# Hybrid decoder trunk: where the FFN's weight sums and work tiles stand in SBUF, the order inside a seven-product chunk, and an eighth seven-product group per layer

## The chip, the core and the metric

The kernel runs on one core of one Trainium2 chip. The metric is the device time of the whole program in microseconds, the median of several runs. One more execution is profiled; its trace is what is read below.

## What is computed

A residual stream x of 256 positions by 2048 features goes through two layers. Layer 0 is a recurrent block (a gated linear recurrence), layer 1 is sliding-window attention with sinks; each is followed by a SwiGLU FFN of width 5632. All of it is float32. The change is about the FFN's first product, `h @ w_in`, which has 2048 rows and 2 x 5632 columns and is made once in each layer:

```python
def swiglu_ffn(x, g, w_in, w_out):
    h = rms_norm(x, g)
    gate, up = jnp.split(h @ w_in, 2, axis=-1)
    return x + (jax.nn.silu(gate) * up) @ w_out
...
for layer in range(DEPTH):
    x = recurrent_block(x, ...) if layer < N_REC else attn_block(x, ...)
    x = swiglu_ffn(x, norm2_g[layer], ffn_w_in[layer], ffn_w_out[layer])
```

## The kernel before, in words

**Jobs.** The weights of every product are cut into blocks of 128 x 1024 floats (512 KB), and each block is one job, here called a chunk: two k-tiles of 128 rows by 512 columns. `stream` (L332) walks over all jobs in order. At job i it issues the load of job i+4 into one of four `raw` tiles, splits job i+3 and emits the matmuls of job i, so the DMAs run four chunks ahead of TensorE and the splits three. `run_bg`, called twice per chunk, lets background generators (norms, activations, the split of the hidden values) emit work as long as a running account of ScalarE's and VectorE's time has room.

**Three products for one.** A float32 product is made as three float32r products. `split` (L303) rounds the weights to `hi` on ScalarE (L311) and takes the rest `lo` on VectorE (L312). The activations are split in the same way into a high and a low half, which lie side by side in a work tile `s`. Each product is then high by high, high by low and low by high.

**Plain chunks.** In `group` (L362, matmuls in `products`, L358) the weights are the stationary operand and the activations the moving one: 24 matmuls of 128x128 by 128x256 in a chunk, 192 in a group of eight chunks. The profile writes them as `b<-s,hi` and `b<-s,lo`: output, then moving operand, then stationary operand. In some chunks (`SYNC`) six of the 256-wide matmuls are replaced by three of 512 columns.

**Seven-product chunks.** In the groups listed in `FAST` (5, 7, ... 17 of the FFN's 22 groups in each layer) the roles are turned round: `fast_group` (L505, matmuls in `put`, L512) has the activations stationary and the weights moving (`b<-hi,s`). In six of the group's eight chunks (`PAIRS`: 0, 1, 2, 4, 5, 6) the 2x2 block product is made with seven block products instead of eight (Winograd's form), 21 matmuls instead of 24. Three of the seven, nine matmuls, take the weights as they are (`old`: moving `hi` or `lo`); four, twelve matmuls, take weight sums (`new`: moving `mh` or `ml`, work tiles, so the profile shows `b<-s,s`). The sums are made ahead by `mix` (L314): three VectorE additions into a tile `d` (L322 to L324), a rounding on ScalarE into `mh` (L325) and a subtraction on VectorE into `ml` (L327), beside the split of three quarters of the raw block (L321, L326). The two other chunks, 3 and 7, are not mixed (`plain` inside `fast_group`); chunk 3 (`RUNS`) has nine 512-wide matmuls and six of 256 columns, chunk 7 has 24 of 256.

**After a seven-product group.** `joined` combines the seven products on VectorE and ScalarE. Its result lies with positions in the partitions, so `turn` transposes it with four matmuls (L711). These wait in `pend` until `flush` is called: in chunk 3 of the next seven-product group, or in chunk 3 of the plain group that follows the last one. That group is the `end` group (18), and after it `split` begins to split the hidden values for the second FFN product.

**Tiles and their places.** All tiles come out of one pool in the order in which they are declared. `hi0` begins at byte 54656 of each partition and `lo0` at byte 71040, both multiples of 128. The thirty work tiles `s0` to `s29`, 4096 bytes each, begin at byte 102336, which is 64 bytes past a multiple of 128, and so do all the others. Work tiles are handed out first in, first out: for activations, sums, scratch and results alike.

Of the kernel before, what the change touches and what calls it, by code (L numbers as in the profile page):

```python
# [17 lines left out]
P = 128  # L18
D = 2048
T = 256  # L20
# [15 lines left out]
K_ONE, K_BLK, K_SEL0, K_SEL1, K_ID = 0, 128, 256, 384, 512  # L36
K_HS, K_MASK = 640, 642
NCON = 642 + 384


class Val:
# [7 lines left out]
class Trunk:  # L49
# [22 lines left out]
    def __init__(self, ctx, tc, dram):  # L72
        self.tc, self.nc, self.d = tc, tc.nc, dram
        nc = self.nc
        const = ctx.enter_context(tc.tile_pool(name="const", bufs=1))
        psum = ctx.enter_context(tc.tile_pool(name="psum", bufs=1, space=bass.MemoryType.PSUM))
        tmp = ctx.enter_context(tc.tile_pool(name="tmp", bufs=1))
        self.tmp = tmp
# [4 lines left out]
        self.whole = deque((i, 0) for i in range(30))  # L83
        self.stamp = 0
        self.part = {F32: deque(), F32R: deque()}
        self.spool = const
        self.held = {}
        self.raw = [const.tile([P, 1024], F32, name=f"raw{i}") for i in range(4)]
        self.hi = [const.tile([P, 1024], F32R, name=f"hi{i}") for i in range(4)]
        self.lo = [const.tile([P, 1024], F32R, name=f"lo{i}") for i in range(4)]  # L90
        self.sets = [[psum.tile([P, 512], F32, name=f"b{4 * i + j}") for j in range(4)] for i in range(2)]
        self.banks = deque(b for q in self.sets for b in q)
        self.misc = 0
        self.started = False
        self.tmps = deque(const.tile([P, T], F32, name=f"t{i}") for i in range(4))
        self.halves = deque(const.tile([P, T], F32, name=f"h{i}") for i in range(4))
        self.rstd = [const.tile([P, T + 2], F32, name=f"rstd{i}") for i in range(2)]
        self.acc = const.tile([P, T], F32, name="acc")
        self.sq = deque(const.tile([P, T], F32, name=f"sq{i}") for i in range(2))
        self.zero = const.tile([P, P + T], F32R, name="zero")  # L100
# [41 lines left out]
        self.nc.vector.reciprocal(out, a)  # L142


    def double(self, dt=F32R):
        i, _ = self.whole.popleft()
        s = self.spool.tile([P, 4 * T], dt, tag=f"s{i}", name=f"s{i}")
        self.held[id(s)] = (i, s)
        return s

    def halved(self, s):
        i, _ = self.held.pop(id(s))
# [5 lines left out]
            out.append(v)  # L158
        return out

    def slot(self, dt=F32R):
        part = self.part[dt]
        if part and (not self.whole or part[0][2] <= self.whole[0][1]):
# [5 lines left out]
        at = self.whole[0][1]  # L169
        a, b = self.halved(self.double(dt))  # L170
        rec = self.held.pop(id(b))[0]
        rec["free"].add(1)
        part.appendleft((rec, 1, at))
        return a

    def room_for(self, dt=F32R):
        return len(self.part[dt]) + 2 * len(self.whole)

    def free(self, s):
        self.stamp += 1  # L180
        rec = self.held.pop(id(s))
        if len(rec) == 2:
            self.whole.append((rec[0], self.stamp))
            return
        rec, h, v = rec
        part = self.part[v.dtype]
        rec["free"].add(h)
        if len(rec["free"]) == 2:
            mate = next(q for q in part if q[0] is rec)
            part.remove(mate)  # L190
            self.whole.append((rec["i"], self.stamp))
        else:
            part.append((rec, h, self.stamp))

# [119 lines left out]
    def mix(self, i, raw, hi, lo):  # L314

        act, tt = self.nc.scalar.activation, self.nc.vector.tensor_tensor
        d = self.double(F32)
        mh, ml = self.double(), self.double()
        two = lambda ap: ap.rearrange("p (a c) -> p a c", c=T)
        q = slice(T, 4 * T)  # L320
        act(hi[:, q], raw[:, q], AF.Copy)  # L321
        tt(two(d[:, 0:2 * T]), two(raw[:, T:3 * T]), raw[:, 0:T].unsqueeze(1).to_broadcast([P, 2, T]), ALU.subtract)  # L322
        tt(d[:, 2 * T:3 * T], raw[:, 2 * T:3 * T], d[:, 0:T], ALU.add)
        tt(d[:, 3 * T:4 * T], raw[:, 3 * T:4 * T], d[:, 2 * T:3 * T], ALU.subtract)  # L324
        act(mh[:, :], d[:, :], AF.Copy)  # L325
        tt(lo[:, q], raw[:, q], hi[:, q].bitcast(F32), ALU.subtract)  # L326
        tt(ml[:, :], d[:, :], mh[:, :].bitcast(F32), ALU.subtract)  # L327
        self.free(d)
        self.mixed[i] = (mh, ml)
        self.dve += self.MORE  # L330

# [173 lines left out]
    def fast_group(self, src, xn, mx, g, done, final):  # L505
# [66 lines left out]

# [3 lines left out]
    def ffn(self, l, xs, r, gains, rn, col, out=None):  # L576
# [8 lines left out]
        def normed():  # L585
# [1 line left out]
                yield 1  # L587
            rs = self.rstd[r][:, 0:T]
            for p in range(8):
                while len(self.whole) < 4:  # L590
                    yield 1
                n, d = self.slot(F32), self.double()
                for j in range(2):
# [28 lines left out]
        def split():  # L622
            for p in range(NH // 2):
                while not raws[p].ready:
                    yield 1
                while len(self.whole) < 2:
# [15 lines left out]
        for g in range(NH // 2):  # L642
# [86 lines left out]
            if g == 0:  # L729
                def begin():  # L730
                    self.spawn(normed())
                    self.DEBT = self.OWED
                self.jobs[-8] = self.with_(self.jobs[-8], begin)
        n = len(self.jobs)
        self.project(self.d[f"ffn_out{l}"], NH, hid, gains, rn, out)

        def end():
            self.DEBT = Trunk.DEBT
        self.jobs[n] = self.with_(self.jobs[n], end)

    def with_(self, job, first):
# [507 lines left out]

    def run(self):  # L1250
        nc, d = self.nc, self.d
        const = self.tmp
        self.nm = const.tile([P, T + 2], F32, name="nm")
        self.nt = const.tile([P, T + 2], F32, name="nt")
        self.r2 = const.tile([P, 2], F32, name="r2")
        self.rrs = [const.tile([P, 48], F32, name=f"rr{i}") for i in range(2)]
# [90 lines left out]
```

## Time and profile before

| what | value |
|---|---|
| time, median of 3 runs | 1990.62 us (1990.02 to 1996.79) |
| the profiled execution's own time | 1994.55 us |
| its span, first to last instruction | 1992.4 us |
| granted TensorE clock | 1.000 |
| TensorE matmuls | 1982.9 us busy, 16487 |
| TensorE weight loads | 1935.5 us busy, 16487 |
| VectorE | 1458.5 us busy |
| ScalarE | 1123.0 us busy |
| DMA | 376.56 MB, 189 GB/s |

Matmuls are pipelined: a row of the profile gives a matmul some 280 ns, while the next one begins after a good 110. What counts for the time is the distance from one start to the next, so the prediction works with differences of start times. In the chain of work that ended last a piece's length is such a difference already.

### The profile page before, as it was taken

How to read it: one execution, taken by the hardware profiler on the slowest of the kernel's cores; microseconds unless marked ns; L12 is line 12 of the kernel's file. 1: busy time of each engine (PE TensorE's matmuls, PEld its weight loads, DVE VectorE, ACT ScalarE, POOL GpSimd, SP SyncE). 2: the span in 40 equal slices, each digit the busy share in tenths (PEclk: the TensorE clock that was granted, in tenths of full speed). 3: DMA queues.
4: the chain of work that ended last, by engine and by line, in shares of the span. 5: the costliest groups of instructions: out<-in, count | busy, mean ns of one | idle time of the engine just before them, and what ended most of it. 6: DMA issues, size and time to landing. Idle time of an engine off the chain costs nothing. (4 is left out here: it accounts for less than half of the span.)

```text
span 1992.4 us, 39949 instructions
## 1 busy us (share of the span) xinstructions
PE 1982.9 (100%) x16487; PEld 1935.5 (97%) x16487; DVE 1458.5 (73%) x2319; ACT 1123.0 (56%) x1626; POOL 0.2 (0%) x4
## 2 busy tenths in 40 slices
PE   9999999999999999999999999999999999999999
PEld 9999999999999999999998789999999999999999
DVE  8989868788888955555677776697888888444543
ACT  7788756555555744444556775564555556444342
POOL 0000000000000000000000000000000000000000
PEclk9999999999999999999999999999999999999999
DMA  7555655655566565555554334565655655556663
GB/s 267 194 188 180 201 191 180 202 198 194 199 201 199 196 196 197 191 191 201 192 181 154 111 128 150 189 191 190 203 201 196 198 196 197 187 190 204 208 202 128
DMA packets 105015, 376.56 MB, mean 189 GB/s; under 512 B 11648, under 2 KB 13824, under 8 KB 104832
## 3 DMA queue, kind: packets, MB, share of 16 engines
q1 hardware_dynamic: 104544, 373.60, 56.6%
q8 instruction: 129, 2.11, 0.4%
q14 instruction: 54, 0.44, 0.1%
q10 hardware_dynamic: 288, 0.40, 0.1%
HBM read 371.86 MB, written 2.10 MB: 188 GB/s over the span
## 5 line engine op out<-in xcount | busy, mean ns | idle before, releaser
L358 PE MATMUL b<-s,hi 128*128 128x256 f32 (+1 forms) x8455 | 1128.5, 280 | 1.6 <-ACT s L118 1.2
L312 DVE TENSOR_TENSOR lo<-raw,hi 128x1024 fp32r<-128x1024 f32 (+1 forms) x621 | 755.9, 1220 | 435.7 <-ACT hi L311 421.2
L358 PEld LDWEIGHTS b<-s,hi 128*128 128x128 f32 x8455 | 1051.7, 188 | 14.2 <-ACT s L118 2.0
L311 ACT ACTIVATE hi<-raw 128x1024 fp32r<-128x1024 f32 (+1 forms) x621 | 654.2, 1056 | 590.5 <-PE b L358 475.0
L358 PE MATMUL b<-s,lo 128*128 128x256 f32 x4352 | 647.1, 277 | 0.0
L358 PEld LDWEIGHTS b<-s,lo 128*128 128x128 f32 x4352 | 564.7, 188 | 0.1
L512 PE MATMUL b<-hi,s 128*128 128x256 f32 (+1 forms) x868 | 163.0, 292 | 0.0
L325 ACT ACTIVATE s<-s 128x1024 fp32r<-128x1024 f32 x84 | 89.2, 1062 | 108.6 <-DVE s L324 107.8
L512 PEld LDWEIGHTS b<-hi,s 128*128 128x128 f32 x868 | 130.4, 189 | 3.8
L512 PE MATMUL b<-s,s 128*128 128x256 f32 x1008 | 133.3, 281 | 0.0
L512 PEld LDWEIGHTS b<-s,s 128*128 128x128 f32 x1008 | 125.2, 189 | 0.0
L327 DVE TENSOR_TENSOR s<-s,s 128x1024 fp32r<-128x1024 f32 x84 | 102.7, 1222 | 20.1 <-ACT s L325 19.9
L512 PE MATMUL b<-lo,s 128*128 128x256 f32 (+1 forms) x434 | 114.1, 289 | 0.0
L118 ACT ACTIVATE s<-s 128x512 fp32r<-128x512 f32 (+3 forms) x172 | 83.0, 519 | 18.4 <-DVE s L127 13.1
L321 ACT ACTIVATE hi<-raw 128x768 fp32r<-128x768 f32 x84 | 70.3, 843 | 35.1 <-issue 21.8
L1232 PE MATMUL b<-hi,s 128*128 128x512 f32 x256 | 84.0, 408 | 0.0
L326 DVE TENSOR_TENSOR lo<-raw,hi 128x768 fp32r<-128x768 f32 x84 | 79.9, 951 | 0.0
L512 PEld LDWEIGHTS b<-lo,s 128*128 128x128 f32 x434 | 76.4, 188 | 1.8
L127 DVE TENSOR_TENSOR s<-s,s 128x512 fp32r<-128x512 f32 (+2 forms) x143 | 74.0, 549 | 4.4 <-ACT s L118 4.4
L322 DVE TENSOR_TENSOR s<-raw 128x512 f32<-128x512 f32 x84 | 57.7, 686 | 12.4 <-DMA raw<-in_ffn_in 12.3
L118 ACT ACTIVATE s<-b 128x256 fp32r<-128x256 f32 (+4 forms) x112 | 49.9, 480 | 25.9 <-PE b L1128 7.9
L1232 PEld LDWEIGHTS b<-hi,s 128*128 128x128 f32 x256 | 45.8, 189 | 9.6 <-issue 1.4
(117 smaller groups left out, 1098.6 us busy)
## 6 DMA issues: line engine op xcount, KB each, us to landing
raw<-in_ffn_in SPq DMA_DIRECT2D x352, 512.0 KB, 3.3
raw<-in_ffn_out SPq DMA_DIRECT2D x176, 512.0 KB, 3.3
raw<-in_lru_in SPq DMA_DIRECT2D x63, 512.0 KB, 3.8
raw<-in_lru_out SPq DMA_DIRECT2D x32, 512.0 KB, 3.4
raw<-in_w_q SPq DMA_DIRECT2D x32, 512.0 KB, 3.2
raw<-in_w_o SPq DMA_DIRECT2D x32, 512.0 KB, 3.3
raw<-in_gate SPq DMA_DIRECT2D x8, 512.0 KB, 4.0
raw<-in_kv SPq DMA_DIRECT2D x8, 512.0 KB, 3.2
```

Of the source, the lines that this page charges most:

```text
L118: self.nc.scalar.activation(out, in_, func, **kw)
L127: self.nc.vector.tensor_tensor(out, a, b, op)
L311: self.nc.scalar.activation(hi[:, q], raw[:, q], AF.Copy)
L312: self.nc.vector.tensor_tensor(lo[:, q], raw[:, q], hi[:, q].bitcast(F32), ALU.subtract)
L321: act(hi[:, q], raw[:, q], AF.Copy)
L322: tt(two(d[:, 0:2 * T]), two(raw[:, T:3 * T]), raw[:, 0:T].unsqueeze(1).to_broadcast([P, 2, T]), ALU.subtract)
L325: act(mh[:, :], d[:, :], AF.Copy)
L326: tt(lo[:, q], raw[:, q], hi[:, q].bitcast(F32), ALU.subtract)
L327: tt(ml[:, :], d[:, :], mh[:, :].bitcast(F32), ALU.subtract)
L358: self.nc.tensor.matmul(ps[f][:, 0:c1 - c0], w, x2[k][:, c0:c1], start=f not in begun, stop=last and all(q[1] != f for q in todo[n + 1:]))
L512: nc.tensor.matmul(st["ps"][b][:, h % 2 * T:(h % 2 + n) * T], x, w, start=b not in st["begun"], stop=True, skip_group_check=True)
L1232: nc.tensor.matmul(st[g][b][:, :], x, q, start=c + kt == 0 and x is xh and q is wh, stop=c == 7 and kt == 1 and q is wl)
```

## The change

It has four parts.

1. **Places.** The tiles are declared in another order, a `pad` is put in and the DMA scratch is cut from 16384 to 2048 bytes a partition. `hi0` now begins at byte 47232 and `lo0` at 63616, multiples of 128 as before. There are 33 work tiles instead of 30, in two kinds. `s0` to `s7` (`NEAR`) begin at byte 91264, a multiple of 128 like the weights. After a `step` of 64 bytes `s8` to `s32` begin at byte 124096, 64 bytes past a multiple of 128. `pool` says which kind a request gets: near tiles for `d`, for the scratch of `joined` and for the weight sums of chunks 1, 2, 5 and 6; the others for the rest, as long as there are any (`a or b`). Outside the FFN's first product scratch tiles take whichever kind has been free longer; inside it (`keep`) they take a near one only when nothing else is left.
2. **Chunks 0 and 4** (`EVEN`) keep their weight sums in the other kind, 64 bytes off, and do the twelve `new` matmuls first and the nine `old` ones after them. `flush` comes in chunk 4 instead of chunk 3.
3. **Chunk 3** has 24 matmuls of 256 columns; the 512-wide ones of `fast_group` are gone. Those of `SYNC` in `group` stay.
4. **`FAST`** goes to 19: eight seven-product groups in each layer instead of seven. The `end` group is 20 instead of 18.

```diff
+PAD = 152 + 32
...
-    FAST = tuple(range(5, 18, 2))
+    FAST = tuple(range(5, 20, 2))
     PAIRS = (0, 1, 2, 4, 5, 6)
-    RUNS = 3
+    EVEN = (0, 4)
     OWED = 9000.0
+    NEAR = 8
...
+        self.whole = [deque((i, 0) for i in range(self.NEAR, 33)), deque((i, 0) for i in range(self.NEAR))]
...
+        for i in range(33):
+            if i == self.NEAR:
+                const.tile([P, 16], F32, name="step")
+            const.tile([P, 4 * T], F32, tag=f"s{i}", name=f"s{i}")
...
+    def pool(self, dt, near):
+
+        a, b = self.whole
+        if near:
+            return b or a
+        if dt == F32 and a and b and not self.keep:
+            return a if a[0][1] <= b[0][1] else b
+        return a or b
...
     def mix(self, i, raw, hi, lo):
 
         act, tt = self.nc.scalar.activation, self.nc.vector.tensor_tensor
-        d = self.double(F32)
-        mh, ml = self.double(), self.double()
+        d = self.double(F32, True)
+        near = self.jobs[i][2] == 1
+        mh, ml = self.double(near=near), self.double(near=near)
...
-            narrow = lambda q: [(q[0] + e, q[1], q[2][:, e * T:e * T + T], 1) for e in range(2)]
-            full = lambda q: [(*q, 2)]
-            if c == self.RUNS:
-                n = narrow(wide[3]) + narrow(wide[4]) + narrow(wide[5])
-                todo = sum(map(full, wide[0:3]), []) + n[0:1] + sum(map(full, wide[6:9]), []) + n[1:2]
-                todo += sum(map(full, wide[9:12]), []) + n[2:]
-            else:
-                todo = sum(map(narrow, wide), [])
+            todo = [(h + e, x, w[:, e * T:e * T + T]) for h, x, w in wide for e in range(2)]
...
             todo = ((5, part(a, 0), old(1)), (3, part(b, 0), old(3)), (2, com(3), old(2)),
                     (7, com(0), new(0)), (6, com(2), new(1)), (4, com(1), new(2)), (1, part(b, 1), new(3)))
+            if c in self.EVEN:
+                todo = todo[3:] + todo[:3]
...
-                if c == self.RUNS:
+                if c == self.EVEN[1]:
                     self.flush()
                 (fast if c in self.PAIRS else plain)(c, hi, lo)
                 if c == 7:
                     done(st["ps"])
-            self.jobs.append((src(c), mm, c in self.PAIRS))
+            self.jobs.append((src(c), mm, (c in self.PAIRS) + (c in self.EVEN)))
...
-                p1, c, u, h = self.half(), self.double(F32), self.slot(F32), self.slot(F32)
+                p1, c, u, h = self.half(), self.double(F32, True), self.slot(F32, True), self.slot(F32)
...
-    nc = bacc.Bacc("TRN2", target_bir_lowering=False, num_devices=1)
+    nc = bacc.Bacc("TRN2", target_bir_lowering=False, num_devices=1, dynamic_dma_scratch_size=2048)
```

The rows below are matmuls in TensorE's order: output bank, moving operand, stationary operand. The first number of a name is the tile's, so `s2` is one of the near tiles in the changed program; the second is the build's running number.

First place, chunk 0 of the second seven-product group of the first layer. Before, the weights come first and the sums (here `s22` and `s17`) after them:

```order
L512 MATMUL b6_89<-hi0_75,s16_3900 128x256 x2
L512 MATMUL b6_89<-lo0_79,s16_3900 128x256
L512 MATMUL b5_88<-hi0_75,s16_3900 128x256 x2
L512 MATMUL b5_88<-lo0_79,s16_3900 128x256
L512 MATMUL b5_88<-hi0_75,s23_3929 128x256 x2
L512 MATMUL b5_88<-lo0_79,s23_3929 128x256
L512 MATMUL b7_90<-s22_5212,s23_3929 128x256 x2
L512 MATMUL b7_90<-s17_5213,s23_3929 128x256
```

Now the sums (`s27`, `s17`) come first and the weights follow:

```order
L539 MATMUL b7_141<-s27_5252,s13_3961 128x256 x2
L539 MATMUL b7_141<-s17_5253,s13_3961 128x256
L539 MATMUL b6_140<-s27_5252,s13_3961 128x256 x2
L539 MATMUL b6_140<-s17_5253,s13_3961 128x256
L539 MATMUL b4_138<-s27_5252,s31_3932 128x256 x2
L539 MATMUL b4_138<-s17_5253,s31_3932 128x256
L539 MATMUL b6_140<-hi0_81,s31_3932 128x256 x2
L539 MATMUL b6_140<-lo0_85,s31_3932 128x256
```

Second place, the join of weights and sums in chunk 1 of the same group. Before, moving sums and stationary activations (`s25`, `s7`) are tiles of one kind:

```order
L512 MATMUL b5_88<-hi1_76,s6_3964 128x256 x2
L512 MATMUL b5_88<-lo1_80,s6_3964 128x256
L512 MATMUL b5_88<-hi1_76,s7_3996 128x256 x2
L512 MATMUL b5_88<-lo1_80,s7_3996 128x256
L512 MATMUL b7_90<-s25_5247,s7_3996 128x256 x2
L512 MATMUL b7_90<-s3_5248,s7_3996 128x256
```

Now the sums are in near tiles (`s0`, `s7`) and the activations in `s15` and `s19`, 64 bytes off:

```order
L539 MATMUL b5_139<-hi1_82,s15_3996 128x256 x2
L539 MATMUL b5_139<-lo1_86,s15_3996 128x256
L539 MATMUL b5_139<-hi1_82,s19_4028 128x256 x2
L539 MATMUL b5_139<-lo1_86,s19_4028 128x256
L539 MATMUL b7_141<-s0_5287,s19_4028 128x256 x2
L539 MATMUL b7_141<-s7_5288,s19_4028 128x256
```

Third place, the passage into the last chunk of the plain group before it. Before, the last pair of activations lies in `s8`, a tile like all the others:

```order
L358 MATMUL b2_85<-s13_4317,lo2_81 128x256
L358 MATMUL b3_86<-s13_4317,lo2_81 128x256
L358 MATMUL b0_83<-s8_4432,hi3_78 128x256 x2
L358 MATMUL b0_83<-s8_4432,lo3_82 128x256
L358 MATMUL b0_83<-s8_4432,hi3_78 128x256 x2
```

Now that pair has been given a near tile, `s2`, because nothing else was free, and it meets weights that are placed in the same way:

```order
L385 MATMUL b2_136<-s18_4349,lo2_87 128x256
L385 MATMUL b3_137<-s18_4349,lo2_87 128x256
L385 MATMUL b0_134<-s2_4464,hi3_84 128x256 x2
L385 MATMUL b0_134<-s2_4464,lo3_88 128x256
L385 MATMUL b0_134<-s2_4464,hi3_84 128x256 x2
```

This is so in the last chunk of all groups from 4 to 21, seven-product and plain, and in both layers. In the second layer the activation sums of chunk 6 have a near tile as well.

More of the change, by code (lines that the diff above doesn't have):

```diff
@@ L81, in __init__ @@
         self.cc = const.tile([P, 32], F32, name="cc")
-        self.x = [const.tile([P, 4, T], F32, name=f"x{i}") for i in range(4)]
[L83 to L87, printed above, removed]
+        self.rstd = [const.tile([P, T + 2], F32, name=f"rstd{i}") for i in range(2)]
+        self.nm, self.nt = (const.tile([P, T + 2], F32, name=n) for n in ("nm", "nt"))
+        self.r2 = const.tile([P, 2], F32, name="r2")
+        self.rrs = [const.tile([P, 48], F32, name=f"rr{i}") for i in range(2)]
+        self.zero = const.tile([P, P + T], F32R, name="zero")
+        const.tile([P, PAD], F32, name="pad")
+        self.x = [const.tile([P, 4, T], F32, name=f"x{i}") for i in range(4)]
         self.raw = [const.tile([P, 1024], F32, name=f"raw{i}") for i in range(4)]
@@ L90, in __init__ @@
         self.lo = [const.tile([P, 1024], F32R, name=f"lo{i}") for i in range(4)]
+        self.tmps = deque(const.tile([P, T], F32, name=f"t{i}") for i in range(4))
+        self.halves = deque(const.tile([P, T], F32, name=f"h{i}") for i in range(4))
+        self.sq = deque(const.tile([P, T], F32, name=f"sq{i}") for i in range(3))
+        self.acc = self.sq.popleft()
+        self.whole = [deque((i, 0) for i in range(self.NEAR, 33)), deque((i, 0) for i in range(self.NEAR))]
+        self.stamp = 0
+        self.keep = False
+        self.part = {(d, n): deque() for d in (F32, F32R) for n in (False, True)}
+        self.spool = const
+        for i in range(33):
+            if i == self.NEAR:
+                const.tile([P, 16], F32, name="step")
+            const.tile([P, 4 * T], F32, tag=f"s{i}", name=f"s{i}")
+        self.held = {}
         self.sets = [[psum.tile([P, 512], F32, name=f"b{4 * i + j}") for j in range(4)] for i in range(2)]
@@ L94, in __init__ @@
         self.started = False
[L95 to L100, printed above, removed]
         self.jobs = []
@@ L142, in rcp, with double @@
         self.nc.vector.reciprocal(out, a)
-    def double(self, dt=F32R):
-        i, _ = self.whole.popleft()
+    def pool(self, dt, near):
[5 more added lines that the diff above has]
+        return a or b
+    def double(self, dt=F32R, near=False):
+        i, _ = self.pool(dt, near).popleft()
         s = self.spool.tile([P, 4 * T], dt, tag=f"s{i}", name=f"s{i}")
@@ L149, in double, with back @@
         return s
+    def back(self, i):
+        self.whole[i < self.NEAR].append((i, self.stamp))
     def halved(self, s):
@@ L159, in halved, with slot @@
         return out
-    def slot(self, dt=F32R):
-        part = self.part[dt]
-        if part and (not self.whole or part[0][2] <= self.whole[0][1]):
+    def slot(self, dt=F32R, near=False):
+        part = self.part[dt, near]
+        q = self.pool(dt, near)
+        if part and (not q or part[0][2] <= q[0][1]):
             rec, h, _ = part.popleft()
@@ L168, in slot @@
             return v
-        at = self.whole[0][1]
-        a, b = self.halved(self.double(dt))
+        at = q[0][1]
+        a, b = self.halved(self.double(dt, near))
         rec = self.held.pop(id(b))[0]
+        rec["near"] = near
         rec["free"].add(1)
@@ L176, in room_for, with spare @@
     def room_for(self, dt=F32R):
-        return len(self.part[dt]) + 2 * len(self.whole)
+        return len(self.part[dt, False]) + 2 * self.spare()
+    def spare(self):
+        return sum(map(len, self.whole))
     def free(self, s):
@@ L182, in free @@
         if len(rec) == 2:
-            self.whole.append((rec[0], self.stamp))
+            self.back(rec[0])
             return
         rec, h, v = rec
-        part = self.part[v.dtype]
+        part = self.part[v.dtype, rec.get("near", False)]
         rec["free"].add(h)
@@ L190, in free @@
             part.remove(mate)
-            self.whole.append((rec["i"], self.stamp))
+            self.back(rec["i"])
         else:
@@ L589, in normed @@
             for p in range(8):
-                while len(self.whole) < 4:
+                while self.spare() < 4:
                     yield 1
@@ L625, in split @@
                     yield 1
-                while len(self.whole) < 2:
+                while self.spare() < 2:
                     yield 1
@@ L732, in begin @@
                     self.DEBT = self.OWED
+                    self.keep = True
                 self.jobs[-8] = self.with_(self.jobs[-8], begin)
@@ L738, in end @@
             self.DEBT = Trunk.DEBT
+            self.keep = False
         self.jobs[n] = self.with_(self.jobs[n], end)
@@ L1251, in run @@
         nc, d = self.nc, self.d
[L1252 to L1256, printed above, removed]
         self.rv = {i: Val() for i in range(4)}
```

2 lines of the change are left out of this document (removed).

## Prediction

> **What bounds the kernel now.** I read the busy times first, then the waits, then the chain of work that ended last, and last the timeline of TensorE inside one seven-product group. The busy times:
>
> ```profile
> PE 1982.9 (100%) x16487; PEld 1935.5 (97%) x16487; DVE 1458.5 (73%) x2319; ACT 1123.0 (56%) x1626; POOL 0.2 (0%) x4
> ```
>
> TensorE works through the whole span. The waits (who, for whom, us in total, times, longest) agree: the great ones are ScalarE and VectorE waiting for TensorE or for each other, and the longest that TensorE has is small.
>
> ```profile
> ACT hi L311 <- PE b L358: 475.0, 320, 2.6
> DVE lo L312 <- ACT hi L311: 421.2, 342, 3.9
> ...
> PEld b L1128 <- DVE s L136: 3.0, 7, 0.8
> ```
>
> So time is won or lost by the number of matmuls and by the distance from one start to the next. The chain gives both for the second layer's FFN (start, length, what):
>
> ```profile
> 1383.35 20.38 PE b L512 x165
> 1403.73 21.76 PE b L358 x192
> 1425.49 7.41 PE b L512 x63
> 1432.91 0.44 PE b L711 x4
> 1433.34 12.96 PE b L512 x102
> 1446.31 21.76 PE b L358 x192
> ...
> 1659.17 8.17 PE b L358 x69
> 1667.34 0.44 PE b L711 x4
> 1667.78 92.26 PE b L358 x770
> ```
>
> A plain group is 21.76 us for 192 matmuls, 113.3 ns each. A seven-product group is 20.38 the first time and 7.41 + 0.44 + 12.96 = 20.81 with transposes, which thus cost 0.43. It saves only 0.95 us on a plain one, although it has 18 matmuls fewer (2.04 us; a wide one counts as two), because its own are slower: 7.41 us for 63 is 117.6 ns. Where these 4 ns lie is seen in the timeline of one such group, whose first column is the start:
>
> ```profile
> 1425.33 0.40 PE L512 MATMUL b<-hi,s 128*128 128x256 f32 x2
> ...
> 1426.39 1.59 PE L512 MATMUL b<-s,s 128*128 128x256 f32 x12
> 1427.82 0.40 PE L512 MATMUL b<-hi,s 128*128 128x256 f32 x2
> ...
> 1428.86 1.58 PE L512 MATMUL b<-s,s 128*128 128x256 f32 x12
> 1430.28 0.40 PE L512 MATMUL b<-hi,s 128*128 128x256 f32 x2
> ...
> 1432.74 0.60 PE L711 MATMUL b<-con,s 128*128 128x128 f32 x4
> 1433.10 0.71 PE L512 MATMUL b<-hi,s 128*128 128x512 f32 x2
> ...
> 1435.99 0.40 PE L512 MATMUL b<-hi,s 128*128 128x256 f32 x2
> ...
> 1443.40 0.64 PE L512 MATMUL b<-hi,s 128*128 128x256 f32 x4
> ...
> 1446.14 1.07 PE L358 MATMUL b<-s,hi 128*128 128x256 f32 x8
> ```
>
> From start to start: nine weight products in chunk 0 take 1.06 us (118 ns each). Twelve sum products take 1.43 (119). The next nine weight products, behind the sums, take 1.04 (115.6, and most of that surplus is at their beginning). Sums again 1.42, and so on. Chunk 7, weights only, is 24 in 2.72 us (113.3). So 113.3 ns is the pace when moving and stationary operands are tiles of different kinds (64 bytes apart) and in step; 118 when they are of different kinds but out of step, which lasts as long as nothing disturbs it; 119 and more when both are work tiles of one kind; and a stretch of this last sort puts what follows in step. Chunk 3 is 2.89 us (1433.10 to 1435.99), not 2.72: the wide matmuls gain nothing.
>
> Plain matmuls know the same two paces. Two windows of one chunk each (24 matmuls), the first in group 21, the second in group 18 ahead of its transposes:
>
> ```profile
> 1738.25:1741.08 2.83, 2.83 (x26) 1.00 0.60 185
> 1661.74:1664.46 2.72, 2.72 (x27) 1.00 0.15 60
> ```
>
> At the same clock (1.00) one takes 0.11 us longer. The slow pace begins at the transposes (1667.34) and lasts over 29 chunks up to the second FFN product, about 29 x 0.11 = 3.2 us.
>
> **The change part by part.** *Seven-product group.* Chunk 0 becomes twelve sum products first, 1.43, and nine weight products in step, 1.04: 2.47. Chunks 1 and 2 have all operands 64 bytes apart: 21 x 0.1133 = 2.38 each. Chunk 3 is narrow: 2.72. Transposes 0.43. Chunks 4 to 7 are the same four again. Sum 2 x (2.47 + 4.76 + 2.72) + 0.43 = 20.33, against 20.81; the first of a layer 19.90 against 20.38.
>
> On the wide matmuls a rule of the Trainium skill speaks against the change: "TensorE: Matmul & The Clock Gate", section "Back-to-back issue gap", gives 262 cycles for 256 columns and 518 for 512, so a wide one would save 6 cycles, and taking away 126 of them would cost some 0.3 us in all (estimate from that page). The trace differs: the chunk that holds nine of them is the slower one.
>
> *Eight groups.* In each layer one plain group of 21.76 goes and one of 20.33 comes. A layer then has 19.90 + 7 x 20.33 = 162.21 where it had 20.38 + 6 x 20.81 + 21.76 = 167.00: 4.79 less, 9.6 us over both. The first layer is as regular as the second: its transposes start at 459.6 and come again 42.56 us later, which is 20.81 + 21.76 to 0.01.
>
> ```profile
> L711 PE MATMUL b<-con,s x56: 270/272/273, 459.6 to 1667.5; 128*128 128x128 f32 x56
> ```
> ```profile
> 502.16 0.60 PE L711 MATMUL b<-con,s 128*128 128x128 f32 x4
> ```
>
> *What it gives back.* The order of the changed program shows the last pair of activations in a near tile, placed like the weights, in chunk 7 of groups 4 to 21. Its 24 matmuls then have both operands of one kind. Before has this only with work tiles on both sides: 1.43 us per twelve, so 2.86 instead of 2.72, and 0.02 to come into step after it. The bounds are 0 (no conflict) and 0.19 (the surplus of chunk 3, 2.89 against 2.72, the slowest chunk of before, and the same 0.02). I take 0.16, the nearest row: 18 groups x 2 layers x 0.16 = 5.8 us. In the second layer chunk 6 has twelve such matmuls more, 0.09 in 8 groups: 0.7 us.
>
> *The slow stretch.* In group 20, chunk 7 meets the near tile and should put group 21 in step, and groups 18 and 19 lie before the transposes now. Of the 3.2 us at most four chunks remain (0.4): I take 2.8 as gained, with bounds 0 and 3.2.
>
> *Costed at nothing.* An extra group needs six mixes per layer in the place of six plain splits. These lie beside matmuls. VectorE is busy 18.23 of 20.82 us in a seven-product group and 18.98 of 21.76 in a plain one (third pair of numbers):
>
> ```profile
> 1425.49:1446.31 20.82, 20.82 (x172) 20.41 (x171) 18.23 (x26) 12.05 (x16) 0.00 (x0) 1.00 0.63 211
> 1446.31:1468.07 21.76, 21.76 (x194) 21.76 (x194) 18.98 (x27) 11.14 (x12) 0.00 (x0) 1.00 0.56 186
> ```
>
> The two together leave 5.4 us free in 42.6, and the new pair is only 0.16 us shorter. The tightest sum tile I found is that of chunk 6 of group 15:
>
> ```profile
> 1608.69 1.23 DVE L327 TENSOR_TENSOR s<-s,s 128x1024 fp32r<-128x1024 f32 x1 [1.19 <-ACT s L325]
> ```
> ```profile
> 1612.28 1.58 PE L512 MATMUL b<-s,s 128*128 128x256 f32 x12
> ```
>
> It is ready at 1609.92 and used from 1612.5: 2.6 us to spare. Chunks 0 and 4 now need their sums 1.06 us earlier, but in chunk 4 the chain of mixes is two chunks shorter. The hidden values' `split` starts one plain group ahead of the second FFN product instead of three. The program emits each of its pieces hundreds of matmuls before its use.
>
> *Sum.* -9.6 + 5.8 + 0.7 - 2.8 = -5.9 us. Against the profiled execution (1994.55, of which the span is 1992.4) that is 1988.6. That execution is 3.9 above the median of the runs shown, so on the median 1990.62 it is **1984.7 us**, 0.3% less.
>
> **The rivals.** *The near pair costs nothing.* Then -9.6 - 2.8 = -12.4: 1978.2. For it: before never has both operands on the weights' side. Against: the sums show that two work tiles of one kind collide, and the other kind is its mirror image. Chance 0.14, faster.
>
> *Placement is not the cause.* The 117.6 ns could belong to the form (activations stationary), not to the tiles. Then only the wide matmuls and the extra group count: 126 x 0.1176 + 48 x 0.1133 = 20.26, with transposes 20.69. A layer has 20.26 + 7 x 20.69 = 165.09, 1.9 less, or 3.8 over both, and two of the slow groups go (16 x 0.11 = 1.8): 1985.0. The Trainium skill, "SBUF — State Buffer", section "SBUF: two separate sides", says as much: TensorE's port never waits on anyone. The trace is against it, with one form at 118 and at 113.3 in one group. Chance 0.13, no change that counts, and the time tells it hardly apart from my forecast; the rows would.
>
> *Out of step, slower.* If sums that come first do not put the weights in step (nothing of before begins a chunk with them), all 126 different-kind matmuls of a group run at 118, 0.57 us more, and the following plain group as well, 168 x 4.5 ns = 0.76, since nothing in it disturbs them. That is 2 x (8 x 0.57 + 7 x 0.76) = 19.8, and the 2.8 are not gained: 1990.6 - 3.1 + 19.8 = 2007.3. It decides from the point where nine weight products behind the sums of chunk 0 read 1.06 instead of 1.04. Chance 0.06.
>
> *VectorE falls behind.* Only eight near tiles serve `d`, `mh`, `ml` and the scratch of `joined`, so a mix may have to wait until TensorE has let go of an earlier sum. If that takes over 2.6 us, TensorE waits; at 1 us in each of 16 groups, 1984.7 + 16 = 2000.7. Against: by the program's order no reuse is later than that of `hi`, which waits for TensorE already. Chance 0.04, slower.
>
> **How the numbers follow.** My forecast has 0.58; the 0.05 left are other stretches that change their pace, as likely no change. About 0.5%, ten us, is what a measurement of this kernel can tell from none. Faster: 0.14, and 0.08 from the forecast's own spread, whose edge (1980.7) is 4 us away: 0.22. Slower: 0.06 + 0.04 = 0.10, less 0.02 for weaker forms of both: 0.08. No change: 0.70. The range reaches from the first rival, 1977.5, to half the way up to the slower ones, 1992.0: outside lie about 0.06 below and 0.10 above.
>
> **What would show it.** Right: seven-product groups of some 20.5 us with transposes (20.33 and 0.16), 63-matmul stretches gone; chunks 1, 2, 5 and 6 at 2.38; chunk 7 at 2.86 in both kinds of group, so plain groups at 21.9; group 21 of the second layer at the fast pace. Wrong: chunk 7 at 2.72 (first rival), chunks 1 and 2 at 2.46 (second), plain groups at 22.5 (third), TensorE waiting for `ml` or `lo` (fourth).

## The result, and the profile after

The changed kernel takes 2006.66 us (median of 6 runs, 2004.10 to 2012.36) where the kernel before takes 1993.31 (6 runs): ratio 1.0071, 95% interval 1.0053 to 1.0088. The forecast was 0.3% less, with a range that ended at 1992.0. So it went the other way, and the measured time lies outside.

Busy times and chain of the changed kernel, the same views as before:

```profile
PE 1995.5 (99%) x16585; PEld 1953.5 (97%) x16585; DVE 1493.7 (74%) x2379; ACT 1136.5 (57%) x1640; POOL 0.2 (0%) x4
```
```profile
1392.79 20.14 PE b L539 x174
1412.93 22.67 PE b L385 x192
1435.60 9.95 PE b L539 x87
1445.55 0.44 PE b L733 x4
1445.99 10.21 PE b L539 x87
1456.20 22.67 PE b L385 x192
```

TensorE still bounds the kernel and hardly waits. The seven-product groups are what the prediction said: in the second layer, which these rows show, 20.14 for the first (19.90 and 0.25 forecast) and 9.95 + 0.44 + 10.21 = 20.60 for the others (20.58 forecast; in the first layer 20.50, with 20.49 forecast). The plain groups between them are not: 22.67 us instead of 21.76, where 21.9 was forecast. The timeline shows where the 0.91 us lie:

```profile
1435.44 1.59 PE L539 MATMUL b<-s,s 128*128 128x256 f32 x12
1436.87 0.40 PE L539 MATMUL b<-hi,s 128*128 128x256 f32 x2
...
1437.91 0.39 PE L539 MATMUL b<-hi,s 128*128 128x256 f32 x2
...
1440.29 0.39 PE L539 MATMUL b<-hi,s 128*128 128x256 f32 x2
...
1453.15 0.64 PE L539 MATMUL b<-hi,s 128*128 128x256 f32 x4
...
1456.03 2.05 PE L385 MATMUL b<-s,hi 128*128 128x256 f32 x16
...
1475.83 0.41 PE L385 MATMUL b<-s,hi 128*128 128x256 f32 x2
...
1478.70 0.76 PE L539 MATMUL b<-s,s 128*128 128x256 f32 x5
```

Chunk 0 has its twelve sums in 1.43 us and the nine weight products behind them in 1.04. Chunk 1, from 1437.91 to 1440.29, takes 2.38, as forecast. Chunk 7, with the near pair, takes 2.88 (1453.15 to 1456.03; forecast 2.86). Then the plain group begins, and its first seven chunks take 19.80 us together (1456.03 to 1475.83): 2.83 each, 117.9 ns a matmul, although their operands are of different kinds. The group has come out of the near pair's chunk out of step and stays so, up to its own chunk 7 (2.87).

The same happens behind group 20: its chunk 7 sends group 21 and the head of the second FFN product into the slow pace. Two chunk starts of group 21 in the first layer are 2.82 apart. In the second layer the slow pace goes on to about 1823; from 1826 on chunks begin 2.72 apart:

```profile
761.09 2.05 PE L385 MATMUL b<-s,hi 128*128 128x256 f32 x16
763.91 2.05 PE L385 MATMUL b<-s,hi 128*128 128x256 f32 x16
...
1817.58 2.05 PE L385 MATMUL b<-s,hi 128*128 128x256 f32 x16
...
1825.98 1.98 PE L385 MATMUL b<-s,hi 128*128 128x256 f32 x16
1828.70 1.98 PE L385 MATMUL b<-s,hi 128*128 128x256 f32 x13
```

Some 30 chunks at 0.11 us is 3.3 us in each layer. Before, the second layer had such a stretch (3.2) and the first had none.

Last, the profiled execution of the changed kernel lost time at its start. The gate matmuls begin 2.8 us later:

```profile
L847 PE MATMUL b<-s,hi x128: 275/276/384, 77.1 to 188.4; 128*128 128x256 f32 x128
```
```profile
L871 PE MATMUL b<-s,hi x128: 276/276/385, 79.9 to 191.2; 128*128 128x256 f32 x128
```

Here TensorE waited 2.3 us for VectorE at 36.5, and its granted clock reads 0.71 from 35 to 40 us and 0.95 from 40 to 45, where it is 1.00 before. In E1, E3, E9 and E11 the gate matmuls begin at 75.9 to 76.2, so the changed tiles do not bring this loss with every execution. Three of the six runs of the changed kernel have a mean clock of 0.998 or 0.999 and are the longest, 2007.41 to 2012.36; the three at 1.000 take 2004.10 to 2005.91, still more than every run of the kernel before. Whether the change makes this start likelier is open.

The account: the span rose by 13.6 us (1992.4 to 2006.0) where -5.9 was forecast, 19.5 apart. Fourteen plain groups at 22.67 instead of 21.92 are 10.5; the second layer's slow stretch, not gained, 2.9; the first layer's new one 3.3; the start 2.8. That is 19.5. It comes out so exactly by some luck: the first chunks of group 20, 8.47 us where they were 8.17, are not in it, 0.3 in each layer.

### The profile page after: what moved, and what is told of

Its sections match the earlier page's. It is cut to its first block, busy times and chain, and to the rows that moved or that the text cites. A ratio compares the mean times of both kernels' runs of the same rounds, so it can differ in the third digit from the quotient of the medians.

```text
span 2006.0 us, 40230 instructions
## 1 busy us (share of the span) xinstructions
PE 1995.5 (99%) x16585; PEld 1953.5 (97%) x16585; DVE 1493.7 (74%) x2379; ACT 1136.5 (57%) x1640; POOL 0.2 (0%) x4
## 5 line engine op out<-in xcount | busy, mean ns | idle before, releaser
L385 PE MATMUL b<-s,hi 128*128 128x256 f32 (+1 forms) x8199 | 1109.2, 282 | 1.9 <-ACT s L127 1.3
L385 PEld LDWEIGHTS b<-s,hi 128*128 128x128 f32 x8199 | 1031.9, 188 | 15.1 <-ACT s L127 2.1
L385 PE MATMUL b<-s,lo 128*128 128x256 f32 x4224 | 633.3, 278 | 0.0
L539 PE MATMUL b<-hi,s 128*128 128x256 f32 x1088 | 182.4, 278 | 0.0
L539 PEld LDWEIGHTS b<-hi,s 128*128 128x128 f32 x1088 | 156.2, 189 | 0.0
L539 PE MATMUL b<-s,s 128*128 128x256 f32 x1152 | 150.2, 280 | 0.0
L539 PEld LDWEIGHTS b<-s,s 128*128 128x128 f32 x1152 | 140.2, 189 | 0.0
L354 DVE TENSOR_TENSOR s<-s,s 128x1024 fp32r<-128x1024 f32 x96 | 117.4, 1223 | 25.0 <-ACT s L352 25.0
L539 PE MATMUL b<-lo,s 128*128 128x256 f32 x544 | 130.5, 278 | 0.0
L539 PEld LDWEIGHTS b<-lo,s 128*128 128x128 f32 x544 | 93.4, 189 | 0.0
L1256 PEld LDWEIGHTS b<-hi,s 128*128 128x128 f32 x256 | 45.8, 189 | 9.5 <-issue 1.4
```

Source lines behind the costliest of these rows:

```text
L385: self.nc.tensor.matmul(ps[f][:, 0:c1 - c0], w, x2[k][:, c0:c1], start=f not in begun, stop=last and all(q[1] != f for q in todo[n + 1:]))
L539: nc.tensor.matmul(st["ps"][b][:, h % 2 * T:(h % 2 + n) * T], x, w, start=b not in st["begun"], stop=True, skip_group_check=True)
L1256: nc.tensor.matmul(st[g][b][:, :], x, q, start=c + kt == 0 and x is xh and q is wh, stop=c == 7 and kt == 1 and q is wl)
```

## The experiments

The theory (A): a near pair of activations in chunk 7 puts the matmuls that follow it out of step, and they stay out. The rival (B): the new order inside the chunks, or the moved transposes, do it. All ratios are to the kernel before, run beside.

**E1, no near pair.** One number is changed:

```diff
-    NEAR = 8
+    NEAR = 6
```

> The changed kernel with NEAR = 6 instead of 8: 27 work tiles are of the other kind, so no pair of activations gets a near tile, in either layer; all else is as changed. Theory A (the near pair in chunk 7 puts the next plain group out of step): plain groups between the seven-product groups 21.76 us instead of 22.67, seven-product groups 20.3 instead of 20.6, the slow stretch ahead of the second FFN product gone; in all some 23 us less than the changed kernel, about 1983 in a profile, 0.995 of before. Theory B (the new order and the moved transposes put it out of step): plain groups stay at 22.67, only the clash in chunk 7 goes (36 times 0.15 us), about 2001, 1.004 of before.

1980.73 us (4 runs), ratio 0.9949, interval 0.9934 to 0.9963: faster than both kernels. The chain:

```profile
1439.58 21.76 PE b L385 x192
1461.34 9.96 PE b L539 x87
1471.31 0.44 PE b L733 x4
1471.74 9.95 PE b L539 x87
```

Plain groups are back at 21.76 and seven-product groups at 9.96 + 0.44 + 9.95 = 20.35, with the new order, the moved transposes and eight groups all in place: A, and within 0.02 us of the forecast 20.33. With six near tiles TensorE waited for a mix once, for some 0.7 us in the first seven-product group of the second layer.

**E2, the near pair alone, in the kernel before.**

```diff
-                n, d = self.slot(F32), self.double()
+                n, d = self.slot(F32), self.other() if p == 7 else self.double()
```

Here `other` gives a tile of its own, declared last, behind a step of 64 bytes; the DMA scratch is cut as in the change to make room for it.

> The kernel before, with one thing of the change: the last pair of normalised activations of each FFN is given a tile of its own that is placed like the weights (64 bytes from the other work tiles). Theory A: the plain groups after a seven-product group go from 21.76 to 22.67 us, chunk 7 takes 2.86 instead of 2.72 in groups 4 to 21, and the time rises by 12 x 0.91 for the plain groups, some 3 for chunk 7 and 3 to 6 for the later plain groups: 15 to 20 us, 1.008 to 1.010. Theory B: only chunk 7 is slower, 36 x 0.15 = 5.4 us, 1.003, plain groups 21.9.

2008.74 us (4 runs), ratio 1.0082 (1.0066 to 1.0099). First seven-product group and the plain group behind it:

```profile
1391.87 20.48 PE b L525 x165
1412.35 22.63 PE b L371 x192
```

One tile, moved by 64 bytes, costs the kernel before 0.8%, in the forecast's range (1.008 to 1.010). Old order, wide matmuls and seven groups are as they were, so B is not needed for the loss.

**E3, both cases in one execution.**

```diff
-                n, d = self.slot(F32), self.double()
+                n, d = self.slot(F32, True), self.double()
...
-                    c, m = self.slot(F32), self.double()
+                    c, m = self.slot(F32, True), self.double()
```

> The changed kernel, in which the scratch of the normalised activations is taken from the near tiles. That leaves tiles of the other kind for all activations in the first layer; in the second the last pair still gets a near tile (the activation sums of chunk 6 do not). One execution then holds both cases. Theory A: plain groups 21.76 us in the first layer and 22.67 in the second, seven-product groups 20.3 and 20.5. Theory B: plain groups 22.67 in both layers.

1991.70 us in one run (1990.67 before). Two chunk starts of a plain group in the first layer, then two in the second:

```profile
476.40 1.98 PE L385 MATMUL b<-s,hi 128*128 128x256 f32 x16
479.12 1.98 PE L385 MATMUL b<-s,hi 128*128 128x256 f32 x16
...
1446.15 2.05 PE L385 MATMUL b<-s,hi 128*128 128x256 f32 x16
1448.98 2.05 PE L385 MATMUL b<-s,hi 128*128 128x256 f32 x16
```

2.72 us in the layer without a near pair, 2.83 in the one with it. A again.

**E4, sums that never clash.** Tiles as in E3, and:

```diff
-        near = self.jobs[i][2] == 1
+        near = True
...
-            if c in self.EVEN:
-                todo = todo[3:] + todo[:3]
```

> As the kernel with the scratch in near tiles, but all weight sums stand in near tiles and chunks 0 and 4 keep the old order (weights first), so that in the first layer every other seven-product group has no stretch in which both operands are of one kind. In the other groups a few single matmuls of chunk 2 have it, and in the second layer the last pair is near. Theory A (nothing puts the weights in step unless such a stretch comes first): 87 matmuls at 118 ns, 10.25 us a half group, in the groups without a stretch, and the plain group behind them at 22.6. Theory B (different kinds run at 113.3 ns by themselves once all operands differ): 9.86 us a half group and 21.76 behind it.

2000.08 us in one run. In the first layer the first seven-product group (5) has no stretch of one kind at all. Twelve sums behind its nine weight products start at 409.86, the next nine weight products at 411.27: 1.41 us, 118 ns, and the plain group behind it (first pair of rows) has the slow pace. The plain group behind the next seven-product group (second pair) is fast:

```profile
409.86 1.58 PE L539 MATMUL b<-s,s 128*128 128x256 f32 x12
411.27 0.40 PE L539 MATMUL b<-hi,s 128*128 128x256 f32 x2
...
432.12 2.05 PE L385 MATMUL b<-s,hi 128*128 128x256 f32 x16
434.95 2.05 PE L385 MATMUL b<-s,hi 128*128 128x256 f32 x16
...
474.83 1.98 PE L385 MATMUL b<-s,hi 128*128 128x256 f32 x16
477.55 1.98 PE L385 MATMUL b<-s,hi 128*128 128x256 f32 x16
```

So tiles of different kinds are not enough. But theory A, that nothing but a stretch of one kind puts the weights in step, does not hold either. Here are the starts of the two seven-product groups that follow (7 and 9), and the transposes of the second:

```profile
451.91 0.40 PE L539 MATMUL b<-hi,s 128*128 128x256 f32 x2
...
452.94 1.52 PE L539 MATMUL b<-s,s 128*128 128x256 f32 x12
...
493.87 0.40 PE L539 MATMUL b<-hi,s 128*128 128x256 f32 x2
...
494.93 1.58 PE L539 MATMUL b<-s,s 128*128 128x256 f32 x12
...
504.12 0.60 PE L731 MATMUL b<-con,s 128*128 128x128 f32 x4
...
504.91 0.39 PE L539 MATMUL b<-hi,s 128*128 128x256 f32 x2
...
505.25 0.39 PE L539 MATMUL b<-hi,s 128*128 128x256 f32 x2
```

Group 7 stands behind the slow plain group and begins in step: nine weight products in 1.03 us, ahead of any sums. Group 9 stands behind a fast plain group and begins out of step (1.06), as group 5 did (408.80 to 409.86). So in this run the pace turned over where the weights change from stationary to moving, and it was carried on where they change back. The first half of group 9 takes 10.25 us up to the transposes. Behind them the pace is the fast one, again ahead of any sums (three weight products in 0.34 us, 504.91 to 505.25), and the half takes 9.96. In the changed kernel the clash in chunks 0 and 4 does set the pace (1.04 behind the sums), but it is one way of several.

**E5, the other side.** Counted by 256 bytes, the weights begin at 128 and the other work tiles at 192. This edit puts them at 64:

```diff
-                const.tile([P, 16], F32, name="step")
+                const.tile([P, 48], F32, name="step")
```

> The changed kernel with the step between near tiles and the others made 192 bytes instead of 64 (48 floats instead of 16). Counted by 128 bytes the two kinds stay 64 apart; counted by 256 bytes the others now lie 64 bytes ahead of the weights instead of behind them. Theory P (only two kinds of place exist): nothing changes, plain groups 22.67, seven-product groups 20.6. Theory Q (it matters on which side the other tile lies, and that is why same-kind work tiles put the next matmuls in step and a near pair does not): the roles are exchanged, plain groups come in step at 21.8 behind the near pair, and seven-product groups run at 118 ns behind their sums, 21.2.

2024.88 us (4 runs), ratio 1.0161 (1.0144 to 1.0178).

```profile
1404.95 20.59 PE b L539 x174
1425.54 21.92 PE b L385 x192
1447.46 10.26 PE b L539 x87
1457.72 0.43 PE b L733 x4
1458.15 10.34 PE b L539 x87
```

The roles are exchanged, as Q said (21.8 and 21.2 forecast). Behind the near pair the plain groups are in step (21.92, its chunk 7 included), and behind the sums the seven-product groups run at 118 ns (21.03 us). Most of the other products run at the slow pace too (192 plain matmuls from 80.19 take 22.61 us, where E1 has 21.76), which is why the whole is slower than the changed kernel. So a same-kind stretch does not put things in step as such: it leaves one of two phases (the same matmuls at 113 or at 118 ns), and which one depends on the side on which the other operand lies.

**E6, old order in chunks 0 and 4.** NEAR = 6, and the two lines of the rotation are taken out.

> The kernel with NEAR = 6 in which chunks 0 and 4 keep the old order, weights first and sums after them; the sums are still 64 bytes off. Theory A: the nine weight matmuls of chunk 0 come out of step behind the plain group (1.06 instead of 1.04 us), the twelve sums put the rest in step, so a seven-product group is 20.3 to 20.4 us and plain groups stay at 21.76; about 1 us over both layers. If the order mattered more, seven-product groups would be at 20.9 and plain groups at 22.6.

1981.50 us in one run; a half group of 87 is 9.97 to 10.00 instead of 9.96, plain groups 21.76. The order itself is worth a few hundredths of a microsecond each time.

**E7, seven groups.** NEAR = 6, and:

```diff
-    FAST = tuple(range(5, 20, 2))
+    FAST = tuple(range(5, 18, 2))
```

> The kernel with NEAR = 6 with seven seven-product groups in each layer instead of eight (FAST up to 17). The prediction priced the eighth group at 21.76 - 20.33 = 1.43 us a layer, so this should be 2.9 us over the kernel with NEAR = 6, if all plain groups that follow the last one are in step; up to 6 more if groups 18 to 21 fall out of step in one layer as they did in the kernel before.

1991.69 us in one run, span 1989.9 against 1978.8 of E1: 11.1 more, where 2.9 to 8.9 was forecast, a miss. Plain groups are 21.76 and half groups 9.96, which fits the priced 1.43 a layer. The rest was not foreseen in this form: groups 18 to 21 are in step, but three chunks in each group of the second FFN product take 2.88 us, the time of a clash (hidden values have been given near tiles), and those behind them 2.83. (In the second layer one such chunk runs from 1782.83 to 1785.71, and the one behind it up to 1788.54.) So the eighth group's price is read from the rows; the time of this run does not test it.

**E8, narrow matmuls in the kernel before.** `todo` in `plain` is built as in the change, and nothing else.

> The kernel before, with the 512-wide matmuls of chunk 3 replaced by 256-wide ones and nothing else. The prediction's price: chunk 3 takes 2.72 us and what the transposes leave behind instead of 2.89, so about 0.1 to 0.17 less in each of 14 groups, 1.3 to 2.4 us in all; plain groups 21.76. The skill's rule on the distance of matmuls gives 0.3 us more instead of less.

```profile
1432.20 12.85 PE b L512 x111
...
1474.66 12.98 PE b L512 x111
```

1993.12 us in one run (1993.46 before): a miss. The half group with chunk 3 takes 12.85 or 12.98 where it took 12.96, and in the first layer all are of the longer sort. In those of 12.98 the narrow matmuls of chunk 3 are out of step behind the transposes (24 in 2.91 us, from 1474.41 to 1477.32). In those of 12.85 they are in step but for the first six, which take 0.79 us instead of 0.68 behind the transposes. In the first seven-product group of a layer, where no transposes come ahead of chunk 3, the edit gains 0.13 (20.25 against 20.38).

**E9, a disturbance at the head of each plain group** of the changed kernel:

```diff
-(0, 3, 4, 5) if end else ()
+(0, 3, 4, 5) if end else (0,)
```

> The changed kernel, near pair and all, in which the plain groups of the FFN (4, 6, ... 18 and 21) begin with three 512-wide matmuls in the place of six 256-wide ones. Theory A says that the slow pace of the plain groups is a state and not a property of their tiles, so a disturbance can end it: as the wide matmuls of the other products do, they put the rest in step, plain groups go from 22.67 to about 21.95 us (21.76, 0.16 for chunk 7 and a little for the wide ones), 14 x 0.7 = 10 us less than the changed kernel, 0.998 to 1.001 of before. If the pace belongs to the tiles, nothing changes: 22.67 and 1.007.

2004.12 us (4 runs), ratio 1.0069 (1.0052 to 1.0086): a miss.

```profile
1410.18 22.66 PE b L385 x189
```

Three wide matmuls do not end the slow pace. The prediction had it that this pace lasts as long as nothing disturbs it; not every disturbance ends it.

**E10, one kind everywhere.** NEAR = 6 and a step of 32 floats, 128 bytes.

> The kernel with NEAR = 6 and a step of 128 bytes, so that all work tiles are placed like the weights and every matmul of the projections has both operands of one kind. If the place of the operands is the cause, nearly all 256-wide matmuls run at 120 ns (the pace of chunk 7 in the changed kernel) instead of 113.3: some 15300 x 6.7 ns = 102 us more than the kernel with NEAR = 6, about 2080. If place is not the cause, 1981 to 1990.

```profile
1486.66 22.78 PE b L385 x192
```

2051.28 us in one run, 70.6 over E1. A plain group is 22.78, 118.6 ns a matmul; I had taken 120. In size this misses (102 forecast), in kind it holds: the same instructions on the same data take 3.6% longer in all when both operands of nearly every projection matmul begin at the same place modulo 128 bytes.

**E11, the near pair elsewhere in its group.**

```diff
-        for c in range(8):
+        for c in (0, 1, 2, 7, 4, 5, 6, 3):
```

> The changed kernel with the chunks of a seven-product group in the order 0, 1, 2, 7, 4, 5, 6, 3 instead of 0 to 7. The same matmuls with the same tiles, the near pair still in chunk 7 of both kinds of group, but in a seven-product group it is followed by the sums of chunk 4, and the plain group follows on chunk 3. Theory A (the near pair does its harm by standing directly ahead of the plain group): plain groups 21.9 us in the first layer instead of 22.67; in the second layer chunk 6 has near activation sums, and whether the 27 matmuls behind them come in step decides. In all 5 to 11 us less than the changed kernel, 1.001 to 1.004 of before. If the harm came from the plain group's own chunk 7, plain groups stay at 22.67 and the time at 1.007.

1999.47 us (4 runs), ratio 1.0047 (1.0030 to 1.0064), a little above the 1.001 to 1.004 of theory A. Chunk starts of a plain group in the first layer and in the second:

```profile
474.88 1.98 PE L385 MATMUL b<-s,hi 128*128 128x256 f32 x16
477.60 1.98 PE L385 MATMUL b<-s,hi 128*128 128x256 f32 x16
...
1452.98 2.05 PE L385 MATMUL b<-s,hi 128*128 128x256 f32 x16
1455.81 2.05 PE L385 MATMUL b<-s,hi 128*128 128x256 f32 x16
```

In the first layer the plain groups are in step again (21.92 us from start to start, 21.9 forecast), although the near pair is still there in both groups: it no longer stands directly ahead, and the clash of chunk 4's sums lies between. In the second layer chunk 6 has near activation sums, and only chunk 3 lies between them and the plain group; the pace stays slow.

## Why the prediction was wrong

**The step that failed** is in "What it gives back": the near pair was charged its own clash "and 0.02 to come into step after it". The clash was right (2.88 and 2.87 against 2.86). What follows was taken from the sums, behind which the weights come in step, and carried over to the weights' side as a mirror image. It is none: behind the near pair 168 matmuls run at 118 ns, 0.75 us a plain group that the sum did not have, 10.5 us in all. They do so when the pair is added (E2), and not when it is taken away (E1) or no longer stands directly ahead (E11, first layer). With the offset on the other side the near pair leaves them in step (E5). The price of a plain group out of step, 168 x 4.5 ns, stood in the prediction's third rival; it was not asked of the near pair.

**The slow stretch** fell with it. Group 20's chunk 7 was to put group 21 in step; it puts it out, in both layers: -2.8 became +3.4.

**What held.** The bound; the three paces as sizes (chunk 7 of the kernel before, read as 2.72, is 2.74 in the prediction's own rows, 1443.40 to 1446.14, with the 0.02 of coming into step); chunk 0 at 2.47, chunks 1 and 2 at 2.38, chunk 7; the seven-product group to 0.1 us; the eighth group's price in the rows of E1 and E7; VectorE, which hid its work but for 0.7 us in E1. The reading that a stretch of one kind puts what follows in step holds for the sums of this kernel and not as a rule (E4, E5). Without the near pair the sum by its own steps would have been -9.6 - 2.8 = -12.4, and E1's span is 13.6 less than before (1978.8 against 1992.4, of which 1.2 at the start). That compares two single executions, and the one of the kernel before is 3.9 above its median; run beside each other, the medians differ by 9.9 us (1980.73 against 1990.67). Where the 3.9 lie is not shown, since no shorter execution of the kernel before was traced; if they are the slow stretch (3.2), the 2.8 were not there to be gained in the shorter runs. The saving was real all the same, and one tile took it back.

**The rivals.** "Out of step, slower" had the right price for a plain group (0.76) and a total of 2007.3 close to what was measured, but another cause: it blamed sums that come first, and its point of decision (1.06 behind the sums) did not come; that read 1.04. Its sign, plain groups at 22.5, came (22.67) for a reason that is not its own, so its total is luck. It had a chance of 0.06. "The near pair costs nothing" fell with E2 and with chunk 7 at 2.88, "Placement is not the cause" with E10, where placement alone costs 70.6 us. The Trainium skill, "SBUF — State Buffer", section "SBUF: two separate sides", says that TensorE (PE) never waits on anyone. It speaks there of engines that share a port; no run here shows TensorE held up at a port by another engine, and E10's loss goes with the places of TensorE's own two operands, so the sentence could not carry this rival. "VectorE falls behind" did not happen in the changed kernel.

**The wide matmuls.** The saving of 2.72 against 2.89 needs chunk 3 to be in step, and 2.89 was read behind the transposes: in the first seven-product group, without them, the wide chunk 3 of the kernel before takes 2.82 (1390.60 to 1393.42). In the changed kernel the narrow chunk is in step; in the kernel before it would not have been in most groups (E8). The Trainium skill, "TensorE: Matmul & The Clock Gate", section "Back-to-back issue gap", gives the cycles that the prediction used as those of an isolated matmul; the estimate from them, 0.3 us in favour of wide ones, is smaller than what E8 can tell.

**Open.** What in the memory makes the phases was not tried. Nor was why the change of roles turns the pace over in E4, or why the transposes sometimes bring the fast pace (E4) and sometimes leave the slow one (E8). Why wide matmuls in other products are followed by the fast pace and those of E9 are not is open as well.

## What to carry to other kernels

When TensorE is bound by matmuls with small moving operands, compare the distance from start to start between groups that do the same work: two values that keep for hundreds of matmuls meant here a phase that was set by what ran before, not a cost of the group itself. Place moving and stationary operands 64 bytes apart modulo 128, time both sides modulo 256 (E5, on the other side, took 2024.88), list from the built program every tile that misses this, and look at what runs behind such a tile, since its own clash is the small part of the price. A pool that falls back to the wrong kind of tile when it runs short should be made to show it.

## What the runs showed of the hardware

- A 128x256 float32r matmul with its weight load has three paces at the full granted clock: 113.3 ns, 117.9 ns with the same operands in the other phase (19.80 us for 168), and 118.6 to 120 ns when both operands begin at the same place modulo 128 bytes (E10: 22.78 us for 192; chunk 7 of the changed kernel: 2.88 for 24).
- Both 113.3 and 117.9 can last for hundreds of matmuls: seven chunks, 168 matmuls, in each plain group, some 30 chunks from group 21 into the second FFN product.
- With no clash between, the pace turned over where weights changed from stationary to moving (E4: 1.06 us for nine behind a fast plain group, 1.03 behind a slow one), and four transposes were followed by the fast pace (E4: a half group of 10.25 us ahead of them, 9.96 behind), but not always (E8: 24 in 2.91 us behind them).
- Modulo 256 bytes the two sides of the weights differ: with the weights at 128 and the other tiles at 192, a stretch of moving sums leaves the fast phase and a near stationary pair the slow one; with the other tiles at 64 it is the reverse (E5: 21.92 for plain groups, 21.03 for seven-product groups).
- Three 512-wide matmuls at the head of a group of 192 do not change the phase (E9: 22.66 against 22.67).
